# Opening of a hybrid layer kernel: plain transposes and a row of 1/rms in the first norm, dt products beside the first two column tiles, three small exponentials as one

## Chip, cores and metric

The kernel runs on one core of one Trainium2 chip. The metric is the device time of one execution in microseconds, the median of several runs. Engines are named as in the profile: PE (TensorE), DVE (VectorE), ACT (ScalarE), POOL (GpSimd), SP (the queue that issues most DMAs).

## What is computed

One layer of a decoder, for 1024 prompt tokens and 8 decode tokens (1032 rows): RMSNorm, one input projection, two groups of heads side by side (HGRN2 and a Mamba-2 SSD mixer), an output projection, then a gated MLP with a short convolution. The part that the change touches is the first norm, the B and C columns and the dt columns of the projection, and the small functions of dt and of the lower bound:

```python
h = rmsnorm(x, w['norm1_w'])
proj = h @ w['w_in']
...
xbc, buf_s_new = causal_dwconv(xbc_r, buf_s, w['ssm_conv_w'], w['ssm_conv_b'])
xbc = jax.nn.silu(xbc.astype(f32))
xs, Bm, Cm = jnp.split(xbc, [D_SSM, D_SSM + SSM_GROUPS * SSM_STATE], axis=-1)
dt = jax.nn.softplus(dt_r.astype(f32) + w['ssm_dt_bias'].astype(f32))
A = -jnp.exp(w['ssm_a_log'].astype(f32))
...
lb_all = jnp.cumsum(jax.nn.softmax(hgrn_lb.astype(jnp.float32), axis=0), axis=0)
```

## The kernel before

Activations are kept transposed, with features on partitions: `hT_hi[k]` and `hT_lo[k]` (tiles `hh` and `hl`) are the eight 128-feature blocks of the normed input, split into a rounded high part and a low remainder, each 1032 tokens wide. Every fp32 product is made of three reduced-precision ones (`hh` by `wh`, `hl` by `wh`, `hh` by `wl`) that accumulate in one PSUM bank. The tokens are walked in three chunks of 344, so that one 128-column tile of the projection costs 3 chunks by 8 blocks by 3 = 72 matmuls. `wload` (L180) loads a column tile of weights (`ws`), ACT rounds it (`wh`, L188) and DVE makes the remainder (`wl`, L189); each has two buffers. Product banks (`mm`, and `dt`) have three.

**The opening.** `first_norm` (L106) runs once for each chunk's group of three token tiles (`xt`, 128 tokens each; the ninth holds the 8 decode tokens). ACT squares and sums each tile in two halves (L115), DVE and ACT make 1/rms (L116 to L118), DVE multiplies an identity matrix by it (`dg`, L119). PE then multiplies each 128 by 128 block of `xt` by `dg` as an fp32 matmul, which transposes and scales in one (`tp`); such a matmul stands as two instructions in the trace. ACT scales by the norm weight and rounds (`hh`, L128), DVE makes `hl` (L129). After each group come the products of that chunk for two column tiles, one of B and one of C (L399 to L406). ACT copies each finished bank to `ext` (`xbc_evict`, L360), a tile of 1060 columns of which there are two buffers (tag `e`).

**After it.** Conv state rows are transposed (`cst`, L338), more norm vectors too (`vps`, L149). `xbc_close` (L368) makes the causal convolution of a column tile: ACT's Identity (L350), three DVE instructions (L352), then Silu on ACT (L374, L375). For the B and C tiles this is called at L424. Then come 48 `dt` matmuls (L433 to L438) into `dtr`, nine fp32 matmuls `dps` that turn dt back to tokens on partitions (L448), and on DVE a chain of some two dozen small instructions for softplus (`spx`, L464 to L480, with one Exp at L469), which ends with `av` (L484). PE needs `av` for `cps` (L486), the running sums of the SSD scan, from which the decay tiles `dec` and `csT` and the whole scan follow. Two more small Exps stand at L482 (`alog_bc`) and L757 (`lbt`). Four masks `lowf` are cut by POOL (L415) in a tile of tag `e`, and DVE copies them to `mlow` (L533).

**Order.** In the opening, on all engines, a scheduler of the framework orders the instructions by their dependences and its own costs, across the calls above. From L1122 on PE's order is the written one: the column tiles of the first x job (`x0`, weights `wh`, bank after bank) and so on to `x3`, `x7`, then the heads, the output projection and the MLP. The other engines stay with the scheduler.

## Time and profile before

| what | value |
|---|---|
| median of 3 runs | 1798.19 us (1797.17 to 1802.01) |
| profiled execution, first to last instruction | 1794.6 us |
| granted PE clock over it | 0.992 |
| busy: PE, DVE, ACT, POOL | 1741.0, 1116.6, 789.1, 409.8 us |
| HBM traffic | 100 GB/s over the span |

The page gives the busy time of each engine, its course over 40 slices, and the costliest groups of instructions. The timeline gives each instruction's start, its duration and, in brackets, the idle time before it and what ended that. Instructions of one engine overlap: a 344-wide matmul is shown with 0.32 us, but the next one starts 0.16 us later. The sum of what PE does is therefore read from starts, not from durations. The profiled span and the median of the runs differ by 3.6 us, which lie around the span.

### The profile page before, as it was taken

Reading aid. Unit: us, or ns where it says so; the run is one execution under the profiler, and the core shown is the slowest. Engines: PE = TensorE matmul, PEld = TensorE weight load, DVE = VectorE, ACT = ScalarE, POOL = GpSimd, SP = SyncE. Lnnn points to the kernel's source line nnn. Section 1 sums busy time; section 2 is a strip of 40 time slices with the busy share of each in tenths; the row PEclk is TensorE's granted clock in tenths of the full one; section 3 lists DMA queues with packets and bytes.
Section 4 is the critical chain, followed back from the end, with each engine's and each line's share of the span. In section 5 each row is a group of like instructions: output and inputs, shape, how many; then the busy total and the mean of one; then the engine's idle time right before and its main releaser. Section 6 shows DMA issues by size and latency. Waiting matters only on the chain.

```text
span 1794.6 us, 38584 instructions
## 1 busy us (share of the span) xinstructions
PE 1741.0 (97%) x16215; PEld 1685.0 (94%) x16215; DVE 1116.6 (62%) x2002; ACT 789.1 (44%) x1414; POOL 409.8 (23%) x415
## 2 busy tenths in 40 slices
PE   7999899999999999999999988999999999999998
PEld 7998798999999999999999978999999999999997
DVE  4658967556555564557746769666666667555545
ACT  6477688454544444345323344333433334111114
POOL 1103331110110110110100364455444542000001
PEclk9999999999999999999999998999999999999999
DMA  5135634553222221235334431222222225422212
GB/s 154 36 98 155 171 100 138 175 147 99 72 77 63 78 79 50 74 96 159 94 107 130 133 116 48 94 73 71 75 85 90 72 71 193 150 95 96 96 60 95
DMA packets 218018, 182.34 MB, mean 102 GB/s; under 512 B 13388, under 2 KB 195158, under 8 KB 217830
## 3 DMA queue, kind: packets, MB, share of 16 engines
q1 hardware_dynamic: 217558, 179.80, 32.5%
q8 instruction: 127, 2.08, 0.5%
q14 instruction: 45, 0.37, 0.1%
q0 software_dynamic: 288, 0.10, 0.0%
HBM read 141.53 MB, written 38.52 MB: 100 GB/s over the span
## 4 chain that ended last, share of the span: by engine, by line
PE 77%; DVE 8%; ACT 6%; DMA 5%; issue 2%; POOL 2%; SPq 0%; DVEq 0%; POOLq 0%; ACTq 0%
PE mm L93 30%; PE ub L93 14%; PE dn L93 13%; PE ua L93 10%; PE a L93 2%; PE o L93 1%; DMA csb<-cs_d 1%; ACT csb L549 1%; PE tp L93 1%; DVE wl L189 1%; DMA Bb<-bc_d 1%; PE kv L93 1%; DMA Sd<-in_state_ssm_dram 1%; DMA out_dram<-Sd 1%; DVE xbc L352 1%
## 5 line engine op out<-in xcount | busy, mean ns | idle before, releaser
L93 PE MATMUL mm<-hh,wh 128*128 128x344 f32 x1248 | 406.2, 326 | 2.6 <-ACT sz L685 2.6
L93 PE MATMUL mm<-hl,wh 128*128 128x344 f32 x1248 | 403.9, 324 | 0.0
L93 PE MATMUL mm<-hh,wl 128*128 128x344 f32 x1248 | 402.8, 323 | 0.0
L93 PEld LDWEIGHTS mm<-hh,wh 128*128 128x128 f32 x1248 | 234.6, 188 | 5.9 <-ACT sz L685 2.9
L93 PEld LDWEIGHTS mm<-hh,wl 128*128 128x128 f32 x1248 | 234.9, 188 | 2.4 <-issue 1.2
L93 PEld LDWEIGHTS mm<-hl,wh 128*128 128x128 f32 x1248 | 234.6, 188 | 2.5 <-issue 0.9
L188 ACT CAST wh<-ws 128x1024 fp32r<-128x1024 f32 x96 | 100.6, 1048 | 265.4 <-PE dn L93 135.8
L93 PE MATMUL ub<-ul,wh 128*128 128x258 f32 x704 | 199.6, 284 | 4.2 <-DVE ul L1182 4.2
L93 PE MATMUL ub<-uh,wh 128*128 128x258 f32 x704 | 201.1, 286 | 2.0 <-ACT uh L1181 2.0
L93 PE MATMUL ub<-uh,wl 128*128 128x258 f32 x704 | 200.8, 285 | 0.0
L93 PE MATMUL dn<-ah,wh 128*128 128x256 f32 (+1 forms) x640 | 180.7, 282 | 1.2 <-DVE x L1425 1.2
L93 PE MATMUL dn<-al,wh 128*128 128x256 f32 (+1 forms) x640 | 180.3, 282 | 0.0
L93 PE MATMUL dn<-ah,wl 128*128 128x256 f32 (+1 forms) x640 | 179.9, 281 | 0.0
L93 PE MATMUL mm<-mh,wh 128*128 128x258 f32 x512 | 148.2, 290 | 10.7 <-DVE x L1078 8.1
L189 DVE TENSOR_TENSOR wl<-ws,wh 128x1024 fp32r<-128x1024 f32 x96 | 125.3, 1306 | 52.5 <-ACT wh L188 52.3
L93 PE MATMUL ua<-ul,wh 128*128 128x258 f32 x528 | 148.9, 282 | 0.9 <-DVE ul L1182 0.9
L93 PE MATMUL ua<-uh,wl 128*128 128x258 f32 x528 | 149.4, 283 | 0.0
L93 PE MATMUL ua<-uh,wh 128*128 128x258 f32 x528 | 149.2, 282 | 0.0
L93 PE MATMUL mm<-ml,wh 128*128 128x258 f32 x512 | 146.5, 286 | 0.0
L93 PE MATMUL mm<-mh,wl 128*128 128x258 f32 x512 | 146.1, 285 | 0.0
L93 PEld LDWEIGHTS ub<-ul,wh 128*128 128x128 f32 x704 | 134.6, 191 | 4.9 <-DVE ul L1182 4.9
L93 PEld LDWEIGHTS ub<-uh,wh 128*128 128x128 f32 x704 | 134.2, 191 | 2.5 <-ACT uh L1181 2.5
(331 smaller groups left out, 3925.0 us busy)
## 6 DMA issues: line engine op xcount, KB each, us to landing
ws<-in_w_in_dram SPq DMA_DIRECT2D x52, 512.0 KB
ws<-in_w_up_dram SPq DMA_DIRECT2D x44, 512.0 KB
ws<-in_w_out_dram SPq DMA_DIRECT2D x24, 512.0 KB
act_d<-val SPq DMA_DIRECT2D x22, 516.0 KB
al<-act_d SPq DMA_DIRECT2D x22, 516.0 KB
ws<-in_w_down_dram SPq DMA_DIRECT2D x22, 512.0 KB
ml<-mix_d SPq DMA_DIRECT2D x48, 172.0 KB
csb<-cs_d SPq DMA_DIRECT2D x32, 256.0 KB
```

The lines of the kernel that those rows point to most:

```text
L93: PE.matmul(out, lhsT, rhs, start=start, stop=stop)
L188: A.copy(wh[:, :n], ws[:, :n])
L189: V.tensor_tensor(wl[:, :n], ws[:, :n], wh[:, :n].bitcast(F32), op=ALU.subtract)
L352: V.scalar_tensor_tensor(acc[:, :n], ext[:, q:q + n], col(wname, q * ntile + j), acc[:, :n], op0=ALU.mult, op1=ALU.add)
L549: A.activation(csb3[:, h, :], csb3[:, h, :], AF.Relu, scale=-1.0, bias=cst[:, h0 + h:h0 + h + 1])
```

## The change

**First norm.** `first_norm` goes. `turned` transposes a block of `xt` with the plain identity (`PE.transpose`), which needs no 1/rms. `Group` holds one chunk's statistics: the squares of the three tiles go to one tile, and sum, root, reciprocal and `dg` (three diagonals in one 128 by 384 instruction) are made once for a group. `rows` multiplies a matrix of ones by the diagonals: each row of the result `rb` holds 1/rms along the tokens, and ACT copies it to SBUF. `normed` multiplies the transposed block by the norm weight and by that row on DVE (`hn`), ACT rounds it to `hh`, and `low` subtracts on DVE (`hl`).

**dt.** The dt weights are loaded earlier (on SP ahead of token tiles 4 to 8), and the 16 dt matmuls of a chunk stand beside the products of the two column tiles (`products`); for the first chunk the products with `wl` and dt are held back three steps. The halves of `wl` are made between the steps of the norm.

**Order.** The whole opening is written out for PE, ACT and DVE. Step s turns block s, norms block s - 3 and multiplies block s - 4, over the 24 blocks of the three chunks.

**Exponentials.** The inputs of the three Exps are laid side by side in one tile of 176 columns with one Exp. The convolution of B and C (`xbc_close`) is issued only after that Exp; its Silus come 52 ticks of the job machine later. `sel`, `mlow`, `eyec`, `ones_r` and `selod` are issued only after the last `hl`.

```diff
-    def first_norm(tiles, then=()):
-
-        xs = []
-        for i in tiles:
-            xt, t0, n = xtm[i]
-            sq = half("xn")
-            ss = keep.tile([P, 4], F32, tag="ss", bufs=4, name=nm("ss"))
-            dg = tl("z", "dg")[:, :P]
-            for i in range(2):
-                A.activation(sq[:n], xt[:n, i * 512:(i + 1) * 512], AF.Square, accum_out=ss[:n, i:i + 1])
-            V.tensor_tensor(ss[:n, 2:3], ss[:n, 0:1], ss[:n, 1:2], op=ALU.add)
-            A.activation(ss[:n, 3:4], ss[:n, 2:3], AF.Sqrt, bias=epsc[:n], scale=1.0 / DM)
-            V.reciprocal(ss[:n, 3:4], ss[:n, 3:4])
-            V.tensor_scalar(dg[:n, :n], ident[:n, :n], ss[:n, 3:4], None, op0=ALU.mult)
-            xs.append((xt, dg, t0, n))
-        for work_ in then:
-            work_()
-        c0, c1 = xs[0][2], xs[-1][2] + xs[-1][3]
-        for k in range(KT):
-            tp = bank("tp")
-            for xt, dg, t0, n in xs:
-                mm(tp[:, t0 - c0:t0 - c0 + n], xt[:n, k * P:(k + 1) * P], dg[:n, :n])
-            A.activation(hT_hi[k][:, c0:c1], tp[:, :c1 - c0], AF.Copy, scale=col("n1", k))
-            V.scalar_tensor_tensor(hT_lo[k][:, c0:c1], tp[:, :c1 - c0], col("n1", k),
-                                   hT_hi[k][:, c0:c1].bitcast(F32), op0=ALU.mult, op1=ALU.subtract)
...
+    ones = keep.tile([P, P], F32, name="ones")
+    G.memset(ones, 1.0)
...
-        A.copy(ext[:, 3 + cs.start:3 + e], ps[:, :e - cs.start])
+        evicted[0] = A.copy(ext[:, 3 + cs.start:3 + e], ps[:, :e - cs.start])
...
-    def xbc_close(j, ext):
+    def xbc_close(j, ext, wait=0):
...
-        A.activation(acc[:, :T], acc[:, :T], AF.Silu)
-        A.activation(acc[:, T:NT], acc[:, T + 3:T + 32:4], AF.Silu)
+
+        def silu():
+            with tc.issue_after(evicted[0].ins):
+                A.activation(acc[:, :T], acc[:, :T], AF.Silu)
+                A.activation(acc[:, T:NT], acc[:, T + 3:T + 32:4], AF.Silu)
+
+        if wait:
+            after(wait, silu)
+        else:
+            silu()
...
+    wdt_s = tl("ld", "wdt_s")[:, :KT * 16].rearrange("p (k m) -> p k m", m=16)
+    wdt = tl("d", "wdt", F32R)[:, :KT * 32].rearrange("p (k m) -> p k m", m=32)
+    load_x(3)
+    SP.dma_start(wdt_s, w_in_[0, :, OFF_DT:OFF_DT + 16].rearrange("(k p) m -> p k m", p=P))
+    for i in range(4, 9):
         load_x(i)
     vec_cols(0)
-    for c in range(NCH):
-        first_norm(range(3 * c, 3 * c + 3), () if c else rounded)
-        for j, w, ext in first:
-            xbc_evict(j, ext, c, chunks[c], prod(w, 0, P, hT_hi, hT_lo, chunks[c]))
-
-
-    ones = keep.tile([P, P], F32, name="ones")
-    G.memset(ones, 1.0)
+    dtr = tl("g", "dtr")
+    G.memset(dtr[:, :NT], 0.0)
+
+    LAG = 4
+    NS = NCH * KT
...
+        def square(self, i):
+            xt, t0, n = self.tiles[i]
+            junk = half("xn")
+            for q in range(2):
+                A.activation(junk[:n], xt[:n, q * 512:(q + 1) * 512], AF.Square, accum_out=self.sq[:n, q, i:i + 1])
...
+        def stats(self):
+            ss = self.ss
+            V.tensor_tensor(ss[:, 0:3], self.sq[:, 0, 0:3], self.sq[:, 1, 0:3], op=ALU.add)
+            A.activation(ss[:, 0:3], ss[:, 0:3], AF.Sqrt, bias=epsc, scale=1.0 / DM)
+            V.reciprocal(ss[:, 0:3], ss[:, 0:3])
+            self.dg = tl("z", "dg").rearrange("p (a t) -> p a t", t=P)
+            V.tensor_tensor(self.dg, ident.unsqueeze(1).to_broadcast([P, 3, P]),
+                            ss[:, 0:3].unsqueeze(2).to_broadcast([P, 3, P]), op=ALU.mult)
+
+        def rows(self):
+            rb = bank("rb", "nx")
+            for i, (xt, t0, n) in enumerate(self.tiles):
+                mm(rb[:, t0 - self.c0:t0 - self.c0 + n], ones[:n], self.dg[:n, i, :n])
+            self.rows_ = tl("z", "rows")
+            A.copy(self.rows_[:, :self.w], rb[:, :self.w])
...
+    def turned(s):
+        g, k = groups[s // KT], s % KT
+        tps[s] = bank("tp")
+        for xt, t0, n in g.tiles:
+            PE.transpose(tps[s][:, t0 - g.c0:t0 - g.c0 + n], xt[:n, k * P:(k + 1) * P], ident[:n, :n])
+
+    def low(u):
+        g, k = groups[u // KT], u % KT
+        return V.tensor_tensor(hT_lo[k][:, g.cs], hns.pop(u), hT_hi[k][:, g.cs].bitcast(F32), op=ALU.subtract)
+
+    def normed(u):
+        g, k = groups[u // KT], u % KT
+        hn = half("hn")[:, :g.w]
+        V.scalar_tensor_tensor(hn, tps.pop(u)[:, :g.w], col("n1", k), g.rows_[:, :g.w], op0=ALU.mult, op1=ALU.mult)
+        A.copy(hT_hi[k][:, g.cs], hn)
+        hns[u] = hn
+        if u:
+            low(u - 1)
...
+    beside = {0: lambda: weight_high(1), 1: lambda: weight_low(0, 0), 2: lambda: weight_low(1, 0),
+              3: dt_weight, 4: lambda: weight_low(0, 1), 5: lambda: weight_low(1, 1)}
...
+        if c == 0 and k < KT - 1:
+            now = [(0, 0), (1, 0), (0, 1), (1, 1)]
+            held.append((k, [(0, 2), (1, 2), (2, 0), (2, 1)]))
+            for w in now:
+                first_mm(c, w, k, k == 0 and w[1] == 0, False)
+            if len(held) > 3:
+                kk, ws_ = held.pop(0)
+                for w in ws_:
+                    first_mm(c, w, kk, kk == 0 and w == (2, 0), False)
+            return
+        for i, ws_ in enumerate(parts):
+            for kk, hw in held:
+                for w in hw:
+                    if w[0] == i:
+                        first_mm(c, w, kk, kk == 0 and w == (2, 0), False)
+            for w in ws_:
+                first_mm(c, w, k, k == 0 and w[1] == 0, k == KT - 1 and w == ws_[-1])
+            if k == KT - 1:
+                if i < 2:
+                    xbc_evict(first[i][0], first[i][2], c, chunks[c], accs[i])
+                else:
+                    A.copy(dtr[:32, chunks[c]], accs[2])
...
+    with tc.manual_schedule(engines={mybir.EngineType.PE, mybir.EngineType.Activation, mybir.EngineType.DVE}):
+        groups.append(Group(0))
+        for i in range(3):
+            groups[0].square(i)
+        groups[0].stats()
+        weight_high(0)
+        for s in range(NS + LAG):
+            if s < NS:
+                turned(s)
+            u = s - LAG + 1
+            if 0 <= u < NS:
+                c, k = divmod(u, KT)
+                if k == 0:
+                    groups[c].rows()
+                normed(u)
+                if u in beside:
+                    beside[u]()
+                if c + 1 < NCH:
+                    if k == 1:
+                        groups.append(Group(c + 1))
+                    if k in (1, 3, 4):
+                        groups[-1].square((1, 3, 4).index(k))
+                    if k == 5:
+                        groups[-1].stats()
+                if u == NS - 1:
+                    settled = low(u)
+            if s >= LAG:
+                products(s - LAG)
...
-    BT[0], CT[0] = (xbc_close(j, ext) for j, w, ext in first)
...
+    with tc.issue_after(settled.ins):
+        V.tensor_tensor(sel, ident[:, 0:16], ident[:, 16:32], op=ALU.add)
...
+    xx, ee_al, s1, s2 = (tl("z", "spx")[:, :NDT + 32] for i in range(4))
+    V.tensor_tensor(lbt[:, 0, :], vcol[:, lo0:lo0 + 8], vcol[:, lo1:lo1 + 8], op=ALU.max)
+    V.tensor_tensor(ee_al[:, NDT + 16:NDT + 24], vcol[:, lo0:lo0 + 8], lbt[:, 0, :], op=ALU.subtract)
+    V.tensor_tensor(ee_al[:, NDT + 24:NDT + 32], vcol[:, lo1:lo1 + 8], lbt[:, 0, :], op=ALU.subtract)
+    V.tensor_copy(ee_al[:, NDT:NDT + 16], alog_bc)
+    xx, ee, s1, s2 = (t[:, :NDT] for t in (xx, ee_al, s1, s2))
...
+    least = V.tensor_tensor(ee, ee, xx, op=ALU.min)
+    expd = A.activation(ee_al, ee_al, AF.Exp)
+    with tc.issue_after(least.ins), tc.issue_after(expd.ins):
+        BT[0], CT[0] = (xbc_close(j, ext, 52) for j, w, ext in first)
+    V.tensor_scalar(alog_bc, ee_al[:, NDT:NDT + 16], -1.0, None, op0=ALU.mult)
+    V.tensor_tensor(lbt[:, 3, :], ee_al[:, NDT + 16:NDT + 24], ee_al[:, NDT + 24:NDT + 32], op=ALU.add)
+    V.reciprocal(lbt[:, 3, :], lbt[:, 3, :])
+    V.tensor_tensor(lbt[:, 0, :], ee_al[:, NDT + 16:NDT + 24], lbt[:, 3, :], op=ALU.mult)
+    V.tensor_scalar(lbt[:, 1, :], lbt[:, 0, :], -1.0, 1.0, op0=ALU.mult, op1=ALU.add)
...
-    A.activation(alog_bc, alog_bc, AF.Exp)
-    V.tensor_scalar(alog_bc, alog_bc, -1.0, None, op0=ALU.mult)
...
-    V.tensor_tensor(lbt[:, 0, :], vcol[:, lo0:lo0 + 8], vcol[:, lo1:lo1 + 8], op=ALU.max)
-    V.tensor_tensor(lbt[:, 1, :], vcol[:, lo0:lo0 + 8], lbt[:, 0, :], op=ALU.subtract)
-    V.tensor_tensor(lbt[:, 2, :], vcol[:, lo1:lo1 + 8], lbt[:, 0, :], op=ALU.subtract)
-    A.activation(lbt[:, 1:3, :], lbt[:, 1:3, :], AF.Exp)
...
```

**Where instructions move (1).** DVE at the seam between the first and the second chunk of tokens. `hl_9` to `hl_16` are the low parts of blocks 0 to 7, `hn` the normed block ahead of its split; `rows_50` and `rows_77` hold the rows of 1/rms of the first and the second group. Before:

```order
L129 SCALAR_TENSOR_TENSOR hl_16_96<-tp_52_225,vcol_99,hh_8_88 128x384
L119 TENSOR_SCALAR dg_63_303<-ident_107,ss_62_302 128x128
L116 TENSOR_TENSOR ss_75_411<-ss_75_411 128x1
L118 RECIPROCAL ss_75_411<-ss_75_411 128x1
L116 TENSOR_TENSOR ss_78_420<-ss_78_420 128x1
```

And now, the same place:

```order
L444 SCALAR_TENSOR_TENSOR hn_72_303<-tp_62_240,vcol_99,rows_50_199 128x384
L439 TENSOR_TENSOR hl_14_94<-hn_69_281,hh_6_86 128x384
L444 SCALAR_TENSOR_TENSOR hn_74_319<-tp_65_257,vcol_99,rows_50_199 128x384
L439 TENSOR_TENSOR hl_15_95<-hn_72_303,hh_7_87 128x384
L444 SCALAR_TENSOR_TENSOR hn_78_341<-tp_68_277,vcol_99,rows_77_339 128x384
L439 TENSOR_TENSOR hl_16_96<-hn_74_319,hh_8_88 128x384
```

The last low part of a chunk, `hl_16`, now stands behind `hn_78`, the first instruction that reads the next group's row. That row comes from three matmuls `rb` on PE, which stand behind the products of the block before.

**Where instructions move (2).** ACT around the evictions of x0. `ext_126` (now `ext_147`) takes the three banks of x0; `wh_132_890` (now `wh_153_930`) is the weight tile of x2, in the buffer that x0 reads; `spx` is the Exp; `xbc` written from `ext` is the Identity that begins a convolution. Before:

```order
L374 ACTIVATE xbc_102_585<-xbc_102_585 128x1024
L375 ACTIVATE xbc_102_585<-xbc_102_585 128x8
L469 ACT_TABLE_LOAD
L469 ACTIVATE spx_111_676<-spx_111_676 128x144
L362 COPY ext_126_799<-mm_127_801 128x344
L362 COPY ext_126_799<-mm_128_827 128x344
L188 CAST wh_132_890<-ws_131_889 128x1024
L362 COPY ext_126_799<-mm_129_853 128x336
```

And now:

```order
L588 ACT_TABLE_LOAD
L588 ACTIVATE spx_130_702<-spx_130_702 128x176
L323 ACTIVATE xbc_133_714<-ext_24_131,vcol_99 128x1056
L323 ACTIVATE xbc_134_720<-ext_28_137,vcol_99 128x1056
L164 CAST wh_153_930<-ws_152_929 128x1024
L337 COPY ext_147_835<-mm_148_837 128x344
L337 COPY ext_147_835<-mm_149_863 128x344
L352 ACT_TABLE_LOAD
```

The two Identities of B and C moved behind the Exp, the Silus behind x0's first evictions, and the rounding of x2's weights ahead of those evictions.

**Where instructions move (3).** DVE between dps and the softplus chain. Before, the six conv instructions (`xbc`) stand ahead of the first instruction that reads `dps`:

```order
L352 SCALAR_TENSOR_TENSOR xbc_101_577<-ext_24_129,vcol_99,xbc_101_577 128x1056
L352 SCALAR_TENSOR_TENSOR xbc_102_585<-ext_28_135,vcol_99,xbc_102_585 128x1056
L447 MEMSET dps_109_656 128x16
L533 CAST mlow_761<-lowf_124_756 32x128 x4
L464 TENSOR_TENSOR spx_110_675<-dps_109_656,bias_bc_667 128x144
L758 TENSOR_TENSOR lbt_773<-lbt_773 128x8
L467 TENSOR_SCALAR spx_111_676<-spx_110_675 128x144
```

And now, where the first half of the softplus chain, from `dps` to a reciprocal, stands ahead of the six conv instructions, of which the last two are shown:

```order
L325 SCALAR_TENSOR_TENSOR xbc_133_714<-ext_24_131,vcol_99,xbc_133_714 128x1056
L325 SCALAR_TENSOR_TENSOR xbc_134_720<-ext_28_137,vcol_99,xbc_134_720 128x1056
L594 TENSOR_TENSOR lbt_700<-spx_130_702,lbt_700 128x8
L598 TENSOR_TENSOR spx_131_703<-spx_131_703,spx_130_702 128x144
L595 TENSOR_SCALAR lbt_700<-lbt_700 128x8
L659 CAST mlow_806<-lowf_145_801 32x128
L599 TENSOR_TENSOR spx_132_704<-spx_131_703 128x144
```

The conv now splits the softplus chain in two, and the first `mlow`, which waits for POOL's masks, stands inside the chain.

91 lines of the change are left out of this document (53 added, 38 removed).

## Prediction

> **What bounds the kernel now.** First the page: how much of the span PE has work.
>
> ```profile
> span 1794.6 us, 38584 instructions
> PE 1741.0 (97%) x16215; PEld 1685.0 (94%) x16215; DVE 1116.6 (62%) x2002; ACT 789.1 (44%) x1414; POOL 409.8 (23%) x415
> ```
>
> PE is the bound: a microsecond of work taken off it counts, unless a wait takes its place. Next the windows, stage by stage (length, then busy time of PE, PEld, DVE, ACT, POOL).
>
> ```profile
> 19.50:65.00 45.50, 45.50 (x311) 41.15 (x309) 22.18 (x55) 24.35 (x54) 0.34 (x2) 1.00 0.21 55
> 65.00:120.00 55.00, 55.00 (x352) 54.14 (x351) 31.70 (x70) 36.48 (x58) 4.80 (x14) 1.00 0.21 55
> 120.00:200.00 80.00, 77.45 (x545) 70.94 (x544) 67.05 (x110) 62.07 (x134) 24.76 (x27) 1.00 0.56 160
> 200.00:250.00 50.00, 44.51 (x298) 40.34 (x297) 40.31 (x70) 38.04 (x79) 16.06 (x11) 0.97 0.49 132
> ```
>
> The opening (to about 65) and the x jobs up to 120 keep PE busy without a gap, DVE and ACT only half so. So the change's stage has nothing to win but PE work, and every new wait is a loss. From 120 to 250, 8.0 us of waits follow. Then PE's timeline at the joints (start, duration):
>
> ```profile
> 9.77 2.50 PE L93 MATMUL tp<-dg,xt 128*128 128x128 f32 x10 [3.67 <-DVE dg L119]
> 25.86 4.85 PE L93 MATMUL tp<-dg,xt 128*128 128x128 f32 x42
> 38.91 7.60 PE L93 MATMUL tp<-dg,xt 128*128 128x128 f32 x48
> 59.75 0.32 PE L93 MATMUL dt<-hl,wdt 128*32 128x344 f32 x1
> 59.90 0.32 PE L93 MATMUL dt<-hh,wdt 128*32 128x344 f32 x1
> 63.34 1.19 PE L93 MATMUL dps<-sel,dtr 128*128 128x16 f32 x10
> 64.37 0.40 PE L93 MATMUL mm<-hh,wh 128*128 128x344 f32 x1
> 69.33 0.21 PE L93 MATMUL dps<-sel,dtr 128*8 128x16 f32 x2
> 76.83 0.32 PE L93 MATMUL mm<-hh,wh 128*128 128x344 f32 x1
> 85.66 0.46 PE L93 MATMUL cps<-av,tri 128*128 128x128 f32 x2
> 1760.82 1.91 PE L1450 MATMUL fin<-ident,x 128*128 128x128 f32 x16
> ```
>
> x0 starts at 64.37, and x1 at 76.83 (72 matmuls and the last dps further) without a gap.
>
> **Part one, the norm on PE.** A transposing matmul by `dg` is two instructions, 4.85 / 42 = 0.115 us each, 0.23 together. A plain transpose is one, 1.91 / 16 = 0.12. The first two groups have 48 blocks: 48 x 0.11 = 5.3 us less. The third group takes 7.60 / 8 = 0.95 per block; with four instructions of 0.115, its 8-row tile takes 0.49, of which a transpose saves half or nothing: 8 x (0.23 to 0.48) = 1.8 to 3.8 less. Added: nine `rb` matmuls, 0.23 each and 0.49 for the 8-row one, 2.3. Net about 6 us of PE work less. The 48 dt matmuls move but stay (0.15 apart).
>
> Whether that arrives depends on what paces PE. For that, ACT and DVE rows:
>
> ```profile
> 8.76 0.19 ACT L115 ACTIVATION_READ_ACCUMULATOR xn<-xt 128x1 f32 x1
> 13.45 0.58 ACT L128 ACTIVATE hh<-tp,vcol 128x384 fp32r<-128x384 f32 x1
> 76.88 1.05 ACT L188 CAST wh<-ws 128x1024 fp32r<-128x1024 f32 x1 [3.18 <-PE mm L93]
> 10.94 1.23 DVE L189 TENSOR_TENSOR wl<-ws,wh 128x1024 fp32r<-128x1024 f32 x1 [0.52 <-ACT wh L188]
> 28.54 0.28 DVE L430 TENSOR_TENSOR wdt<-wdt_s,wdt 128x128 fp32r<-128x128 f32 x1
> 30.68 2.88 DVE L129 SCALAR_TENSOR_TENSOR hl<-tp,vcol,hh 128x384 fp32r<-128x384 f32 x5 [0.30 <-ACT hh L128]
> 33.47 0.60 DVE L119 TENSOR_SCALAR dg<-ident,ss 128x128 f32<-128x128 f32 x3
> ```
>
> DVE did one 384-wide instruction a block (2.88 / 5 = 0.58) and now does two. The squares of the third tile end at 8.95; sum, root, reciprocal and a 384-wide `dg` (1.2 in all), `rb` (six instructions at the 0.25 of the first row above), the copy (0.5), the first `hn` and its rounding (1.1) bring the first product to about 13.6. From 12.4 on DVE has, up to the seventh `hl`, 15 x 0.58 + four half `wl` (half of 1.23 each) + `wdt` 0.28 + the next group's statistics 0.9 = 12.3 us: that `hl` is there at 24.7. PE's work in that time is less than 9 us; DVE paces the first chunk. Then the seam: six products (0.95), a block's transposes (0.35), three `rb` (0.7), ACT's copy (0.5), `hn` (0.58), and only then the eighth `hl` (0.58): 28.4 and some handoffs, against PE out of work at about 27. So 1.5 us of wait, and the same at the next seam. The rest: 2.4 us to end the first chunk, then 64 products (0.157) with four old and four new blocks' transposes and `rb` (14 to 16 with the seam's wait 1.5 more), then 64 products with four blocks (11.5 to 13). Last, x0's bank is free only when ACT has done a rounding of 1.05, held until PE's last read of the first `wh`, and evictions behind it: another 0.8. Together x0 starts at 60 to 62; I take 61.2. By my sum most of the 6 us goes into DVE's pace and the two seams.
>
> Equal footing: in x0 now lie all 18 dps instructions (10 took 1.03 before, so 1.85), two groups of four small transposes (0.9 by the 0.12 each) and two vector ones (0.2). x0's PE work is 72 x 0.158 + 2.95 = 14.3, so it ends at 75.5, against 76.83: **-1.3 us**.
>
> **Part two, the seam from x0 to x1.** Rows for the chain behind dps:
>
> ```profile
> 71.98 0.33 ACT L469 ACTIVATE spx<-spx 128x144 f32<-128x144 f32 x1 [1.99 <-DVE spx L468]
> 72.21 0.43 ACT L362 COPY ext<-mm 128x344 f32<-128x344 f32 x1
> 60.03 7.46 DVE L352 SCALAR_TENSOR_TENSOR xbc<-ext,vcol,xbc 128x1056 f32<-128x1056 f32 x6 [0.76 <-ACT xbc L350]
> 70.07 0.93 DVE L533 CAST mlow<-lowf 32x128 uint8<-32x128 f32 x4 [2.49 <-POOL lowf L415]
> 72.34 0.24 DVE L470 TENSOR_SCALAR spx<-spx 128x144 f32<-128x144 f32 x1
> 72.61 1.05 DVE L471 RECIPROCAL spx<-spx 128x144 f32<-128x144 f32 x1
> 74.10 0.31 DVE L473 TENSOR_TENSOR spx<-spx 128x144 f32<-128x144 f32 x1
> 85.20 0.31 DVE L484 TENSOR_TENSOR av<-dt,alog_bc 128x144 f32<-128x144 f32 x1
> L415 POOL TENSOR_SCALAR_AFFINE_SELECT lowf<-ones 128x128 f32<-128x128 f32 x4 | 3.6, 932 | 8.6 <-DVE xbc L352 8.6
> ```
>
> Before, the conv ran from 60.03 to 67.49 under the dt matmuls, both `ext` buffers were free, and x0's first bank left at 72.21, 4.6 us ahead of need. Now the conv waits for the Exp, the Exp for dps, and dps stands 28 products and the small transposes inside x0: it ends 7.4 us after x0's start, at 68.6. Three small DVE steps and the Exp (1.3), three small ones and the reciprocal (1.5) and six conv instructions (7.46) reach 78.9. One `ext` buffer goes to `lowf`; the other comes free with the last conv. ACT, in order, holds all evictions of x0 behind that, and x1's first product needs x0's first bank (three banks). So x1 starts at 78.9 + 0.5 = 79.4, against PE free at 75.5: **+3.9 us**. If the `ext` buffers did not bind, the rounding for x2, which waits for x0's last read and now stands ahead of the evictions, would still cost 1.05 + 0.43 = 1.5.
>
> **Part three, cps.** `lowf` starts with the fifth conv instruction's end, 77.7, and takes POOL 3.6: 81.3. The first `mlow` in DVE's queue waits for it, and the rest of the softplus chain stands behind. From 74.10 to 85.51 that rest took 11.4 before (with x2's `wl` and x0's conv among it, as now): `av` is there at about 92.8. PE comes to cps 56 products after x1's start, 79.4 + 8.8 = 88.2. Before, `av` came 0.15 ahead of cps. Now **+4.6 us**; without the mask in the chain it would be 2.4.
>
> **Part four, the Exps.** One Exp of 176 columns for three; two table loads fewer in the whole program. Their rows:
>
> ```profile
> 28.66 1.28 ACT L482 ACT_TABLE_LOAD   x1
> 29.96 0.21 ACT L482 ACTIVATE alog_bc<-alog_bc 128x16 f32<-128x16 f32 x1
> ```
>
> ACT is half idle there and PE had no gap: 0. [...]
>
> **The sum.** -1.3 + 3.9 + 4.6 = 7.2 us; with x0 at 62.2 it is 8.2, at 60 it is 6.0. All three terms are new waits on chains that follow x0's start. Behind cps, the chain of waits runs over ACT and a load of the running sums that cps makes, and is back on PE at 221:
>
> ```profile
> 85.06 1.28 ACT L374
> 98.31 8.17 DMA csb<-cs_d
> 221.24 11.35 PE mm L93 x72
> ```
>
> So a late cps is mostly passed on; where PE was delayed by more than that chain, up to a us or so is taken back from the 8.0 of waits there. I forecast +6.3: 1794.6 + 6.3 + 3.6 around the span = 1804.5, the median of 1798.2 plus 6.3.
>
> **Rivals.**
> *The waits are absorbed.* PE lost 3.9 at the seam, and meanwhile DVE, ACT, POOL and the loads went on, so that half of the 8.0 us of waits up to 250 go. For it: those waits end on DVE and ACT. Against: these engines wait on cps too. 7.2 - 4 = +3: 1801. Chance 0.22.
> *The opening keeps its 6 us.* DVE does the 384-wide steps faster than its old 0.58 (SBUF alone for `hl`), the seams hide, and the banks do not bind at x1. Then -6 plus the 1.5 of the rounding, -4.5: 1793.7; wholly without waits 1792.2. For it: DVE was half idle in the window from 19.5. Against: the order puts the conv behind the Exp. It decides if the first `ext` of x0 comes before 75.5. Chance 0.13.
> *PE stays at half pace longer.* The transposes before 12.6 took 0.25 each, those from 25.86 on 0.115. In the new order PE starts with transposes and gaps, so the slow pace might last into the products up to 25: about 9 us of work would take up to twice as long, of which DVE's pace hides some 5: +3, in all +9.5: 1807.7. [...] Chance 0.12.
>
> **Numbers.** The forecast has the remaining 0.53. Some 0.3%, 5.4 us, is what a measurement here can tell from no change. The forecast's own range is 1802.5 to 1806.5; a fifth of it lies within the 5.4. Same: 0.10 + 0.20 (absorbed) + 0.04; slower: 0.43 + 0.02 + 0.12; faster: 0.09. The range reaches from the absorbed case's lower side, 1798, to the slow clock's upper, 1809.5.
>
> **What would show it.** Right: PE's first products at 13 to 15; two waits of 1 to 2 us on `hl` at about 27 and 45; x0 at 60 to 62; a wait of about 4 before x1 on ACT's `ext`, that on DVE's conv; one of about 4.6 before cps on `av`; `mlow` waiting for `lowf` inside the chain. Wrong: x1 without a wait, `av` ahead of PE, or the lag at 250 under 3 us.

## The result and the profile after

| | before | after |
|---|---|---|
| median | 1798.33 us (1797.17 to 1802.01, 4 runs) | 1814.97 us (1813.78 to 1817.73, 4 runs) |
| profiled span, granted PE clock | 1794.6 us, 0.992 | 1814.1 us, 0.989 |

The ratio is 1.0089 (95% interval 1.007 to 1.0107): 16 us slower, between 12.6 and 19.3. The forecast was 1804.5, range 1798.0 to 1809.5: the sign was right, the size less than half. In one kernel below (the kernel before with only the second part of the change) two of the twelve executions, of 2399.33 and 6622.31 us, count as slow and are not in its median. The page of the changed kernel has nearly the same PE work (1743.7 against 1741.0) in a span 19.5 us longer, so most of what came is waiting:

```profile
span 1814.1 us, 38478 instructions
PE 1743.7 (96%) x16161; PEld 1684.9 (93%) x16161; DVE 1122.2 (62%) x2014; ACT 785.6 (43%) x1407; POOL 408.5 (23%) x415
```

Its windows (length; busy time of PE, PEld, DVE, ACT, POOL; granted PE clock; DMA share; GB/s):

```profile
19.50:65.00 45.50, 41.80 (x268) 35.87 (x266) 25.26 (x66) 21.84 (x52) 0.00 (x0) 1.00 0.16 44
65.00:120.00 55.00, 47.73 (x280) 46.47 (x280) 34.83 (x74) 29.47 (x47) 5.14 (x16) 0.91 0.19 52
80.00:85.00 5.00, 4.77 (x21) 4.77 (x22) 3.10 (x12) 4.35 (x8) 2.62 (x8) 0.67 0.00 0
95.00:100.00 5.00, 5.00 (x20) 4.94 (x20) 0.72 (x3) 3.67 (x8) 0.00 (x0) 0.50 0.01 3
```

In the second window PE now stands 7.3 us of 55, where it had no gap, and the clock is 0.91 where it was 1.00. The last two rows cut out the stretches where it drops; nothing in the prediction's sum stood for them.

PE's timeline of the changed kernel at the joints (start, duration, in brackets the wait):

```profile
13.86 0.64 PE L93 MATMUL mm<-hh,wh 128*128 128x344 f32 x1
23.64 0.57 PE L93 MATMUL mm<-hl,wh 128*128 128x344 f32 x2 [0.71 <-DVE hl L439]
29.11 0.43 PE L93 MATMUL mm<-hl,wh 128*128 128x344 f32 x1 [1.05 <-DVE hl L439]
46.64 0.43 PE L93 MATMUL mm<-hl,wh 128*128 128x344 f32 x1 [1.11 <-DVE hl L439]
61.52 0.42 PE L93 MATMUL mm<-hh,wh 128*128 128x344 f32 x1 [0.84 <-ACT dtr L503]
80.23 0.65 PE L93 MATMUL mm<-hh,wh 128*128 128x344 f32 x1 [3.58 <-ACT ext L337]
80.68 0.49 PE L93 MATMUL mm<-hl,wh 128*128 128x344 f32 x1
80.97 0.49 PE L93 MATMUL mm<-hh,wl 128*128 128x344 f32 x1
94.39 0.76 PE L93 MATMUL cps<-av,tri 128*128 128x128 f32 x2 [3.68 <-DVE ddx L631]
232.42 0.63 PE L738 MATMUL sT<-ident,S 128*128 128x128 f32 x4 [3.58 <-DVE S L713]
408.08 1.51 PE L93 MATMUL ms<-gacc,ones 128*128 128x344 f32 x2 [2.87 <-DVE vd L959]
871.14 0.75 PE L93 MATMUL a<-q,k 128*32 128x32 f32 x64 [3.89 <-DVE q L992]
1778.36 1.91 PE L1565 MATMUL fin<-ident,x 128*128 128x128 f32 x16
```

x1 (80.23) is 3.4 us later than before, cps (94.39) 8.7. Behind each of the two waits, products start 0.29 us apart (80.68, 80.97) and not 0.16. The last four rows are later than the same instructions of before by 12.0, 13.1, 14.7 and 17.5 us (the first three of these are in the next fence). Before had these there:

```profile
220.39 0.63 PE L613 MATMUL sT<-ident,S 128*128 128x128 f32 x4 [2.00 <-DVE S L588]
394.97 0.85 PE L93 MATMUL ms<-gacc,ones 128*128 128x344 f32 x2 [0.67 <-DVE vd L844]
856.48 0.76 PE L93 MATMUL a<-q,k 128*32 128x32 f32 x64
```

So three waits far behind the change grew as well, by 1.6, 2.2 and 3.9 us. The other engines of the changed kernel at the seam from x0 to x1, and before cps:

```profile
72.28 7.36 DVE L325 SCALAR_TENSOR_TENSOR xbc<-ext,vcol,xbc 128x1056 f32<-128x1056 f32 x6
76.53 1.04 ACT L164 CAST wh<-ws 128x1024 fp32r<-128x1024 f32 x1 [3.35 <-PE mm L93]
79.73 0.79 ACT L337 COPY ext<-mm 128x344 f32<-128x344 f32 x2 [2.16 <-DVE xbc L325]
78.55 3.63 POOL L541 TENSOR_SCALAR_AFFINE_SELECT lowf<-ones 128x128 f32<-128x128 f32 x4 [12.81 <-DVE xbc L325]
82.22 0.23 DVE L659 CAST mlow<-lowf 32x128 uint8<-32x128 f32 x1 [1.54 <-POOL lowf L541]
93.93 0.31 DVE L608 TENSOR_TENSOR av<-dt,alog_bc 128x144 f32<-128x144 f32 x1
```

The conv ends at 79.64 and ACT copies x0's bank at once, which lets x1 start; `lowf` keeps POOL till 82.2, and `mlow`, inside the softplus chain, waits for it. Both chains are those of the prediction.

### The profile page after: what moved, and what is told of

Its sections match the earlier page's. It is cut to its first block, busy times and chain, and to the rows that moved or that the text cites. A ratio compares the mean times of both kernels' runs of the same rounds, so it can differ in the third digit from the quotient of the medians.

```text
span 1814.1 us, 38478 instructions
## 1 busy us (share of the span) xinstructions
PE 1743.7 (96%) x16161; PEld 1684.9 (93%) x16161; DVE 1122.2 (62%) x2014; ACT 785.6 (43%) x1407; POOL 408.5 (23%) x415
## 4 chain that ended last, share of the span: by engine, by line
PE 76%; DVE 9%; DMA 5%; ACT 5%; issue 3%; POOL 2%; SPq 0%; DVEq 0%; POOLq 0%; ACTq 0%
PE mm L93 30%; PE ub L93 14%; PE dn L93 13%; PE ua L93 10%; PE a L93 2%; PE o L93 1%; DMA csb<-cs_d 1%; DVE xbc L325 1%; ACT csb L674 1%; DVE wl L165 1%; PE kv L93 1%; DMA out_dram<-Sd 1%; DMA Bb<-bc_d 1%; POOL Cb L777 1%; ACT L675 0%
## 5 line engine op out<-in xcount | busy, mean ns | idle before, releaser
L93 PE MATMUL mm<-hh,wh 128*128 128x344 f32 x1248 | 411.5, 331 | 5.3 <-ACT ext L337 3.6
```

Source lines behind the costliest of these rows:

```text
L93: PE.matmul(out, lhsT, rhs, start=start, stop=stop)
```

## The experiments

"Lag" is how much later PE starts an instruction than the first profile of the kernel before starts the same one; that profile's execution was some 2 to 4 us quicker than the medians of its kernel (1798.3 to 1800.4 in the batches here): in every execution with both figures the time is 1.65 to 2.35 us above the span, so that the 3.6 us between its 1794.6 and the median do not all lie around the span. Dummy products are products that nobody reads. Theory A at the start: the chains of the prediction are right, and a half pace behind each standstill and later losses come on top. Rivals: the new edge that holds the conv behind the Exp costs by itself, or the mask does.

**The conv at its old place** (B and C, ahead of dps, Silus at once):

```diff
+    BT[0], CT[0] = (xbc_close(j, ext) for j, w, ext in first)
...
-    with tc.issue_after(least.ins), tc.issue_after(expd.ins):
-        BT[0], CT[0] = (xbc_close(j, ext, 52) for j, w, ext in first)
```

> The changed kernel, with the convolution of the B and C tiles issued where it stood before, ahead of dps, and its Silus at once (no waiting for the joint Exp). Theory A (the queues behind dps): the conv no longer waits for the Exp, but the dt products no longer lie behind the opening to cover it. It starts at about 66, with the vectors, so the masks come at about 77, the Exp behind them at 78, and ACT still holds x0's first eviction behind the Exp: the wait before x1 stays 2.5 to 4 us, the one before cps falls from 3.7 to about 2. In all 1 to 3 us less than the changed kernel: 1812 to 1814. Rival B (tying the conv to the Exp is by itself the cause): the wait before x1 goes, and with it 7 to 11 us: 1804 to 1808.

Measured: 1811.65 us, ratio 1.0058 (1.0046 to 1.007). The wait before x1 stays (3.96 us), that before cps falls from 3.68 to 0.65. ACT in this run:

```profile
65.93 2.43 ACT L323 ACTIVATE xbc<-ext,vcol 128x1056 f32<-128x1056 f32 x2 [3.78 <-DVE vcol L124]
79.62 0.35 ACT L589 ACTIVATE spx<-spx 128x176 f32<-128x176 f32 x1 [1.07 <-DVE spx L588]
79.88 1.12 ACT L337 COPY ext<-mm 128x344 f32<-128x344 f32 x3
```

Without the edge the conv's Identity waits for a transposed vector until 65.93, and x0's evictions now stand behind the Exp. `av` comes 1.3 us sooner (92.61), and PE's order now has 66 products between x1 and cps, where the change had 56; the lag at 112 us falls from 11.3 to 5.7. So the edge costs a part of the time behind x1; at x1 itself another chain of the same length takes its place, since the dt products no longer stand there for the conv to hide under. The rival that the edge alone is the cost falls.

**The mask out of the chain** (`mlow` only behind `av`):

```diff
-            V.tensor_copy(mlow[rows], lowf[rows, :, rows])
+            with tc.issue_after(av_.ins):
+                V.tensor_copy(mlow[rows], lowf[rows, :, rows])
```

> The changed kernel, with the four mlow copies issued only after av, so that the softplus chain on DVE does not wait for POOL's masks. Theory A: the wait before x1 stays 3.6 us; the wait before cps falls from 3.7 to 1.5 to 2, and the half-pace stretch of PE behind it (2.5 us lost) goes or halves: 2 to 4.5 us less than the changed kernel, 1810.5 to 1813. Rival (the chain of small DVE instructions is late whatever stands in it): no more than 0.5 us less.

Measured: 1815.66 us, 1.009 (1.0078 to 1.0102). A miss: Theory A's 2 to 4.5 us did not come. The wait before cps is gone, but PE waits a little further on, and the half pace behind x1 is twice as long (granted clock 0.51 from 80 to 85 us and 0.80 to 90, against 0.67 and then 1.00; timeline, then a window of this run):

```profile
98.37 0.18 PE L634 MATMUL dd<-ident,ddx 8*32 8x8 f32 x1 [2.25 <-ACT csT L625]
```

```profile
80.00:85.00 5.00, 4.11 (x14) 4.12 (x15) 4.76 (x13) 4.58 (x8) 4.07 (x6) 0.51 0.30 83
```

**PE kept busy through the two waits** (23 dummy products ahead of x1, 15 about cps; nothing is left out):

```diff
+    def warm(n):
+        wm = bank("wm")
+        for i in range(n):
+            mm(wm[:, :CH], hT_hi[0][:, :P], hT_hi[0][:, chunks[0]])
```

> The changed kernel, with 38 matmuls added whose result nobody reads: 23 ahead of x1's first product and 15 around cps, where PE stood still. They fill the waits and shorten none. Theory A with the clock (a standstill of 3.6 us costs PE's full pace for the next 3.4 or 6.8 us): x1 and cps come within 0.4 us of where they came (80.2 and 94.4), products behind both are 0.158 us apart instead of 0.287, so PE's lag at 100 is 2 to 2.6 us smaller; 1 to 3 us less than the changed kernel: 1812 to 1814. Rival (the half pace comes from elsewhere, or added work costs its time): the half pace stays at 80 and 95, and the kernel takes 0 to 6 us more.

Measured: 1812.36 us, 1.0067 (1.0055 to 1.0079). Its timeline, then its windows:

```profile
77.05 3.69 PE L93 MATMUL wm<-hh 128*128 128x344 f32 x23
80.79 0.42 PE L93 MATMUL mm<-hh,wh 128*128 128x344 f32 x1
...
94.96 0.76 PE L93 MATMUL cps<-av,tri 128*128 128x128 f32 x2 [3.35 <-DVE ddx L638]
```

```profile
80.00:85.00 5.00, 4.95 (x32) 4.68 (x32) 3.10 (x12) 4.66 (x9) 2.96 (x7) 1.00 0.00 0
95.00:100.00 5.00, 5.00 (x25) 4.98 (x26) 0.72 (x3) 4.66 (x9) 0.00 (x0) 0.72 0.00 0
```

Where PE had dummy work instead of a wait, x1 runs at clock 1.00, 32 products in the window where the change had 21. At cps, where the dummies did not close the gap, half the slow stretch remains (clock 0.72 from 95 to 100, against 0.50). So in these two runs the pace goes with the standstill. But it is not a cost everywhere: from x1 to cps PE takes 14.17 us here and 14.16 in the change. In both, as in the kernel before, cps starts 0.46 us behind the start of `av`; at full pace PE only waits longer for it. The lag at 112 us is hardly less than the change's (11.1 against 11.3; x0 came half a microsecond later); that part of the expectation failed.

**The seam** (the last `hl` of a group ahead of the next group's rows):

```diff
-        if u:
+        if u % KT:
...
+                    if c:
+                        low(u - 1)
```

> The changed kernel, with the last low part of a chunk issued ahead of the next group's rows, on DVE and PE, at the two seams of the opening. Theory A: the two waits of 1.1 us on hl go; x0, x1 and cps each come 2 to 2.5 us sooner, since the chain behind dps starts from x0, and the two large waits stay as long as they are: 2 to 2.5 us less, 1812.5 to 1813. Rival C (the conv, the masks or the loads set x1 and cps by times of their own): x0 comes sooner, x1 and cps do not, the large waits grow by 2: within 0.5 us of the changed kernel.

Measured: 1812.36 us, 1.0065 (1.005 to 1.008). The waits on `hl` fall from 2.9 to 0.4, x0 starts at 59.43, and the two waits behind it stay:

```profile
78.14 0.65 PE L93 MATMUL mm<-hh,wh 128*128 128x344 f32 x1 [3.57 <-ACT ext L337]
92.31 0.77 PE L93 MATMUL cps<-av,tri 128*128 128x128 f32 x2 [3.76 <-DVE ddx L633]
```

Both chains hang on x0's start, as the prediction had it: all comes 2.1 us sooner.

**The parts apart.** The first kernel has the dt products behind the two column tiles with the conv under them, but the new norm and the joint Exp; the second is the kernel before with only the joint Exp, the conv behind it and the late Silus; the third is the first with the seam's edit.

```diff
-            held.append((k, [(0, 2), (1, 2), (2, 0), (2, 1)]))
+            held.append((k, [(0, 2), (1, 2)]))
...
+    BT[0], CT[0] = (xbc_close(j, ext) for j, w, ext in first)
+    for c, cs in enumerate(chunks):
+        ps = psmm.tile([P, 512], F32, tag="mm", name=nm("dt"))
+        for k in range(KT):
+            mm(ps[:32, :CH], wdt[:, k, :], hT_hi[k][:, cs], start=(k == 0), stop=False)
+            mm(ps[:32, :CH], wdt[:, k, :], hT_lo[k][:, cs], start=False, stop=(k == KT - 1))
+        A.copy(dtr[:32, cs], ps[:32, :CH])
```

> The changed kernel with the 48 dt products behind the first two column tiles again and the conv of B and C under them, as before; the new first norm, its written-out order and the joint Exp stay. Theory A: the two large waits (before x1 and before cps) go, and with them the half-pace stretches; what is left is the opening alone, in which the 6 us of saved PE work are eaten by DVE's pace in the first chunk and three waits of 1.2 to 1.6 us: x1 starts within 1 us of before (76.8), the kernel takes 0 us more or less than before, within 2. Rival (the new opening saves its 6 us, and the conv and its queues cost 20): 4 to 6 us less than before. Rival (the new opening itself costs): 4 to 10 us more than before.

> The kernel before with only the second part of the change: the joint Exp, the conv of B and C tied behind it and the late Silus; opening and dt stay as they were. Theory A: dps ends at 65 to 66 here, so the same chain ends sooner against x1 (76.8): a wait of 1 to 2 us before x1 and 1 to 2 before cps, no half pace behind waits that short: 2 to 4 us more than before. Rival (the order tied to the Exp costs what the whole change costs): 9 us and more above before. Rival (harmless without the new opening): within 1 us of before.

> The same as the run with the dt products behind, with the last low part of a chunk also ahead of the next group's rows at the two seams. Theory A: the seams give 2 to 2.5 us; x1 starts at 74.5 to 75, and no wait takes their place, so 2 to 2.5 us less than that run, 1 to 3 less than before. Rival C (a wait of fixed time at x1 or cps takes it back): as that run.

Measured: the first 1808.54 us, 1.0041 (1.0023 to 1.0059); the second 1803.88, 1.0019 (1.0002 to 1.0036); the third 1803.92, 1.0017 (1.0002 to 1.0032), against 1799.19 for the kernel before. The first is outside Theory A's 2 us, within the rival's 4 to 10; the third, expected 1 to 3 us below before, is above it. The second fits Theory A, and has both waits, though smaller:

```profile
80.52 0.43 PE L93 MATMUL mm<-hh,wh 128*128 128x344 f32 x1 [1.32 <-ACT ext L364]
93.48 0.46 PE L93 MATMUL cps<-av,tri 128*128 128x128 f32 x2 [2.13 <-DVE ddx L528]
```

So the late conv hurts also where dt stands at its old place; and the half pace that Theory A did not expect there comes behind the wait of 2.13 us (clock 0.71 from 95 to 100). The first shows that the new norm alone wins nothing: between 110 and 140 us its lag is 0.3 to 0.5, its waits on `hl` come to 4.2 us in five. And it shows something that no theory had: without a wait of note up to 140, its lag is 4.0 at 300 us and 9.8 at 1100.

**All repairs together, dt beside the tiles** (the seam's edit, the conv right behind the opening, the mask behind `av`, and the small transposes inside the last chunk):

```diff
+            if s - LAG in (17, 18, 19):
+                next(cols, 0)
+            if s - LAG in (20, 21):
+                vec_cols(s - LAG - 19)
...
+    BT[0], CT[0] = (xbc_close(j, ext) for j, w, ext in first)
```

> The changed kernel with the dt products beside the column tiles, as changed, and three repairs: the last low part ahead of the next group's rows at the seams; the conv state's transposes and the two vector transposes in the written-out order of the last chunk, so that the conv of B and C starts right behind the opening (about 62) and dps ahead of x0; the mlow copies behind av. Theory A: the conv ends at 70, x0's evictions and av come in time; waits of 0 to 1 us before x1 and before cps, x1 at 72 to 73.5 although all of x0's small work is done by then: 3 to 5 us less than before. Rival (the opening is bound by DVE, and more in its last chunk makes it slower): x0 not before 63, no gain over before.

Measured: 1802.24 us, ratio 0.9998 (0.9981 to 1.0014): not told from the kernel before, and 12.7 us below the change by the medians. The 3 to 5 us below before that Theory A expected did not come. The stage that was lost is mended:

```profile
65.00:120.00 55.00, 54.14 (x344) 52.98 (x343) 36.28 (x73) 33.90 (x57) 6.22 (x16) 1.00 0.23 64
```

It is 4.3 us ahead of before at 120 us, level at 400 and 3.3 behind at 1100. What it gains early it loses later, too.

**Is it lateness that loses?** The kernel before once more, unchanged; with 70 and with 20 dummy products between two products of x2, from 100 us on (the expectations say x3 and 115 us), PE's other instructions in their old order; and with the load of the dt weights as early as in the change (`ones` earlier as well).

```diff
+    after(200, lambda: warm(70))
```

```diff
+    load_x(3)
+    SP.dma_start(wdt_s, w_in_[0, :, OFF_DT:OFF_DT + 16].rearrange("(k p) m -> p k m", p=P))
+    for i in range(4, 9):
         load_x(i)
```

> The kernel before once more, unchanged, to learn how far two profiles of one kernel differ along the way. If the later losses of the change (at 160 to 230, 330 to 400 and 860 us) are a matter of chance between executions, this profile shows losses of several us against the first one at some of these places, and its span is 2 us or more longer than 1794.6. If they belong to the change, it stays within 1 us of the first profile all along. Time within 2 us of the other runs of the kernel before.

> The kernel before with 70 products that nobody reads put between two products of x3, at about 115 us, and every instruction else in its old place: TensorE is late by 70 times 0.152 us, about 10.6, as it is in the change at this point. Theory A (lateness alone changes what later transfers and vector steps meet, and these cost another 5 to 8 us): 16 to 19 us over the kernel before, with waits for S, vd and q such as the change shows. Theory B (the later losses come with the change's own instructions or their order): 10 to 11.5 us over, and a lag that stays level from 130 us on. Theory C (other engines have slack and take part of the delay back, as the prediction's third part thought of a microsecond): 6 to 9.

> As the run with 70 unread products, with 20: TensorE 3.0 us late at 115 us. Theory A: 3 us plus some of the later losses, 4.5 to 9 over the kernel before. Theory B: 2.5 to 3.5. Theory C: 0 to 2.

> The kernel before with only the load of the dt weights issued ahead of the fourth and later row tiles, as in the change, and the ones set earlier on GpSimd; the sums and their order on the other engines are as before. Theory B in the form that the order of the early transfers carries the later losses: 4 to 7 us over the kernel before. Theory A: within 1.5 us of it, with x0 at 63 within half a microsecond.

Measured against 1800.35: unchanged 1798.69, 1.0002 (0.9991 to 1.0013); 70 dummies 1813.77, 1.0087 (1.0066 to 1.0108); 20 dummies 1806.14, 1.0036 (1.0021 to 1.0051); the transfers 1799.25, 0.9996 (0.9984 to 1.0008). The dummies put PE 11.1 and 3.15 us back; the kernels are 11.9 to 19.4 and 3.8 to 9.2 us slower (by the medians 13.4 and 5.8). So a kernel with dummies loses more than they take. That this is lateness alone is not shown:

- Both profiles were 2.4 and 2.2 us late before the first dummy product (the unchanged repeat 0.5): the third token tile came 0.6 to 1.0 us later, and the first products, up to 17 us, took another 1.2. That is as much as the medians have above the 11.1 and 3.15; whether every execution of these kernels has it is not known.
- The scheduler gave ACT, DVE and POOL another order between 100 and 257 us, as it did in the change.
- The early dt load costs nothing. But the change also issues two copies of convolution state at 16 and 22 us; in the transfer run, as in the kernel before, they are issued at 28 and 29. The change's whole order of early transfers is not tested.

The lags of all these profiles:

| kernel | lag at 112 us | at the last product |
|---|---|---|
| before, unchanged | 0.5 | 1.5 |
| before, early dt load | 1.0 | 4.0 |
| before, only the second part of the change | 7.5 | 7.3 |
| before, 20 dummies; 70 dummies | 5.3; 13.5 | 11.6; 18.8 |
| the change | 11.3 | 19.0 |
| the change, dt behind; and with the seam's edit | 0.5; -1.5 | 12.4; 7.4 |
| the change, all repairs | -3.1 | 6.0 |

Lateness at 112 us is neither needed for the later losses nor enough for them. The old opening with the late conv is 7.5 us late and loses nothing more. Three kernels with the new opening are on time or ahead and lose 9 to 12; in the two with dt behind, PE, DVE, ACT and POOL run the very order of the kernel before from 112 us on. By the medians these two are 9.3 and 4.7 us above before. So Theory B does not fall: the profiles, one of each kernel, point to something of the new opening that costs time later, and no run here shows what it is. The early state copies are one candidate that is left.

Three of the later waits, one by one. First row, unchanged kernel; second, 70 dummies:

```profile
220.79 0.63 PE L613 MATMUL sT<-ident,S 128*128 128x128 f32 x4 [3.59 <-DVE S L588]
```

```profile
409.84 0.85 PE L93 MATMUL ms<-gacc,ones 128*128 128x344 f32 x2 [3.00 <-DVE vd L850]
```

The changed kernel's 3.58 before `sT` thus comes in the old kernel too, by chance; it needs nothing of the change. Its 2.87 before `ms` comes with 70 dummies (3.00), and with dt behind, at a lag of 2.9 (3.04). And its 3.89 before `a` comes with 20 dummies; here is that run with POOL, DVE and PE:

```profile
859.46 1.04 POOL L863 TENSOR_TENSOR vb<-vb,k 128x512 f32<-128x512 f32 x1 [12.40 <-PE a L93]
859.85 0.69 DVE L885 TENSOR_TENSOR tt<-tt 128x32 f32<-128x32 f32 x1
860.58 1.54 POOL L865 TENSOR_TENSOR Sh<-Sh,vb 128x512 f32<-128x512 f32 x1
860.89 1.26 DVE L885 TENSOR_TENSOR tt<-tt 128x16 f32<-128x16 f32 x1
863.95 1.75 DVE L883 TENSOR_TENSOR q<-q,tt 128x512 f32<-128x512 f32 x1
865.85 1.08 PE L93 MATMUL a<-q,k 128*32 128x32 f32 x64 [3.79 <-DVE q L883]
```

Two small DVE steps end within 0.05 us of the POOL steps that had begun ahead of them. The same steps in the kernel before:

```profile
853.74 0.17 DVE L879 TENSOR_TENSOR tt<-tt 128x32 f32<-128x32 f32 x1
853.84 0.50 DVE L1018 TENSOR_TENSOR ml<-ml,mh 128x344 fp32r<-128x344 f32 x1
853.95 3.01 POOL L857 TENSOR_TENSOR vb<-vb,k 128x512 f32<-128x512 f32 x1 [13.01 <-DMA vb<-vd_d]
854.27 0.16 DVE L879 TENSOR_TENSOR tt<-tt 128x16 f32<-128x16 f32 x1
856.32 0.67 DVE L879 TENSOR_TENSOR tt<-tt 128x8 f32<-128x8 f32 x1
857.34 1.77 DVE L876 TENSOR_TENSOR k<-k,tt 128x512 f32<-128x512 f32 x1
```

There DVE's `tt` of 32 columns began 0.2 us ahead of POOL, and DVE was in its next step (`ml`) when POOL came; it was POOL that took 3.01, against the 1.04 above. DVE steps took longer only later (`tt` of 8 columns 0.67 us, `k` 1.77 against 0.67), where PE did not wait for them. It goes by this order in the six kernels compared for it. PE waits 3.79 to 3.89 us before this `a` in the three where POOL came 0.3 to 0.4 us ahead of that `tt` (20 dummies, all repairs, the change), and at most 1.0 in the three where POOL came 0.2 to 0.8 us behind it (the kernel before, the one with only the second part of the change, the one with dt behind). How late PE is does not decide it: that `tt` comes 2.4 us sooner to 11.3 us later than in the kernel before in the first three, 0 to 7.5 later in the others. With all repairs, 3.1 us ahead just before it, the wait comes too:

```profile
857.32 0.75 PE L93 MATMUL a<-q,k 128*32 128x32 f32 x64 [3.83 <-DVE q L996]
```

**Those POOL steps left out.** The kernel with 20 dummies, the changed one and the one before, each without the four POOL steps of the last HGRN head (`vb` times `k`, `Sh` plus `vb`, twice), so that head's decode state and what comes of it lack a term:

```diff
-                G.tensor_tensor(d4(vb), d4(vb), cb(k[:, ds]), op=ALU.mult)
+                if h < H - 1:
+                    G.tensor_tensor(d4(vb), d4(vb), cb(k[:, ds]), op=ALU.mult)
...
-                G.tensor_tensor(Sd, Sd, vb, op=ALU.add)
+                if h < H - 1:
+                    G.tensor_tensor(Sd, Sd, vb, op=ALU.add)
```

> The kernel before with 20 unread products as in the run before, and without the four GpSimd steps that update the decode state of the last HGRN head (vb times k, Sh plus vb, twice), so that head's sampled state lacks one term. If these steps slow the VectorE chain tt, k, q when they fall on it, the wait of the product a for q at 866 (3.8 us) goes to under 0.5, the chain's tt 128x16 is back from 1.26 to 0.16 us, and the loss between 850 and 870 (4.1 in the profile of the run with the steps) goes; time 2.5 to 4.5 us under that run, so 1 to 4 over the kernel before. If it is something else that comes with the lateness (a transfer, the order), the wait and the 4.1 stay and the time is that of the run with the steps.

> The changed kernel without the same four GpSimd steps of the last head. If they carry the loss at 860: a<-q wait at 871 from 3.9 to under 0.5, lag behind the kernel before from 16.0 to 11 to 13 at 880, time 3 to 5 us under the changed kernel, 1810 to 1812. If not: 1814 to 1816.

> The control: the kernel before without the four steps. There they fell on a k and a q that no product waited for at once; so 0 to 1 us under the kernel before. If leaving them out helps here by 3 or more as well, their cost has nothing to do with the lateness.

Measured against 1799.67: 1802.57, 1.0009 (0.9993 to 1.0025) with 20 dummies; 1813.36, 1.0069 (1.0044 to 1.0095) for the change; 1798.36, 0.9983 (0.9965 to 1.0002) for the kernel before. With 20 dummies:

```profile
859.63 0.16 DVE L887 TENSOR_TENSOR tt<-tt 128x16 f32<-128x16 f32 x1
861.56 0.75 PE L93 MATMUL a<-q,k 128*32 128x32 f32 x64 [0.28 <-DVE q L885]
```

The wait goes from 3.79 to 0.28, and the lag at 880 us from 10.5 to 4.9; there these steps carry the loss. In the changed kernel they carry the wait (q is back to 0.69 us), but the lag at 880 falls only from 16.0 to 14.0, since 2.1 us of other loss came at 850; the expected time, 1810 to 1812, was missed. In the times neither gain is told from none: the intervals overlap with those of the kernels that have the steps.

## Why the prediction was wrong

The prediction's steps, in the order of the timeline:

| step | predicted | measured |
|---|---|---|
| first products | 13 to 15 | 13.86 |
| x0 starts; wait before it | 61.2 (60 to 62); 0.8 | 61.52; 0.84 |
| waits on `hl` | two of 1 to 2 | 1.05 and 1.11, and one of 0.71 |
| part one: PE free for x1, against before | 75.5, -1.3 | 76.65, -0.2 |
| part two: wait before x1; x1 | 3.9; 79.4 | 3.58; 80.23 |
| half pace from x1 to cps | not in the sum | 1.65, within the wait for `av` |
| part three: wait before cps; end of `av` | 4.6; 92.8 | 3.68; 94.24 |
| lag at cps | 7.2 | 8.7 |
| half pace behind cps | not in the sum | 2.5 |
| lag at 112 us | 7.2 | 11.3 |
| from there on | -0.9 | +8.2 in these two profiles, some 5 by the medians |

*What was right.* Parts one to three, as mechanisms: the DVE pace, the seams, the conv behind the Exp, the `ext` buffers, the mask in the chain. The four runs of the first batch moved these waits one by one, and each moved as the chain says, but for the mask's, where the next wait was already there. Part one was 1.1 us too kind, mostly because x0's stage took 15.1 and not 14.3 us.

*First failed step: "The sum".* It has 7.2 us at cps and no cost behind it; measured are 8.7 and 11.3. One part is a term that was too small: the path to `av` took 1.4 us longer than summed, as the conv ended 0.7 late, POOL's masks 0.9, and the rest of the softplus chain took 12.1 and not 11.4 us. The other is a term that the sum put at nothing, since it priced each wait at its length: having stood for 3.68 us, PE came back at half pace (clock 0.50 from 95 to 100 us, products 0.29 us apart). From cps to the same later product (`bc`, at 112 us before) it took 28.87 us without a wait, against 26.34: 2.5 us. In the run with dummy products the pace goes with the standstill: where they filled the gap, at x1, the slow stretch is gone (clock 1.00 from 80 to 85, against 0.67); where 3.35 us of a gap were left, at cps, half of it stays (0.72 from 95 to 100, against 0.50). From x1 to cps PE was slow too (10.48 us without the wait, against 8.83), but that only shortened the wait for `av`, which set cps either way. The rival "PE stays at half pace longer" had this mechanism, but at the start of the kernel, and there it was hidden: the products from 15.2 to 18 did run at half pace (0.29 us apart, from 18.5 on 0.16), under DVE's, and x0 came on time. That rival asked what pace would do in the opening, and never what the forecast's own two waits would do to it. A half pace came behind the waits of 3.58 and 3.68; the run with only the late conv shows one behind a wait of 2.13 too, and the run with the mask moved none behind 2.25 (clock 1.00 from 95 to 105).

*Second failed step: "up to a us or so is taken back".* It took the waits up to 250 for slack. They gave 1.2 us back by 130 (the lag fell from 11.3 to 10.1), but the lag was 13.5 at 240, of which the wait before `sT` is chance. Later places lost more: it rose from 10.9 to 13.8 about `ms`, from 10.7 to 16.0 about `a` (the wait of 3.89 and a half pace of 1.3 behind it, clock 0.60 from 871 to 875), and by 1.4 in the last transposes, with 2.6 and 2.4 given back ahead of `ms` and `a`. The waits further down were thus no slack. What sets them is shown for `a`: whether POOL's steps or DVE's come first, by some tenths of a microsecond; without POOL's steps the wait is gone (0.28 us with 20 dummies). For the rest the cause stays open: a late PE is not it by itself (7.5 us late, and nothing more lost, in the old opening with the late conv), and kernels with the new opening lose 9 to 12 us without it. Also shown is that the first profile of before was a lucky one (its unchanged repeat lagged by 1.5 at the end, and the one with the early dt load by 4.0, with no difference in the times), so that of the 19.5 us some 3 are the two profiles' own. Left open too: what holds `ms`, which no run isolates, and the 2.1 us at 850 in the run of the change without the POOL steps.

*The other rivals.* "Absorbed" fell: nothing was. "The opening keeps its 6 us" fell at its named point: the first `ext` of x0 came at 79.73, not before 75.5. (`hl`, now from SBUF alone, took 0.55 us by its median, 0.61 before.)

## What to carry to other kernels

Price a wait of a PE that has no gap as its length plus any slow stretch that the trace shows behind it, and ask what that stretch meets: here it cost 2.5 us where no wait followed, and nothing where the next wait was longer than it. Ask of each new wait whether other products could stand in it. When work is moved off a place, ask first what it covered there: behind the opening the dt products hid a conv of 7.4 us. And do not count on waits further down to take a delay back. Profile the old kernel twice before later differences are put down to a change, and compare the other engines' orders before a run with dummy work is read as lateness alone.

## What the hardware showed beside that

In the two profiles of the result all eleven stretches at a granted clock of 0.5 that ended within the span lasted 3.41 us or two or three times that. In the changed kernel it stood there from 79.88 to 83.29 us, about x1, and from 93.53 to 100.36, about cps. Within each of the two profiles they also began whole steps of 3.41 us apart: in the changed kernel at 79.88 and 233.48, 45 steps. It went by how much of one step PE stood idle: from 20 us on, up to the last 30, a step at clock 1.00 was always followed by a slow one when PE had stood 1.92 us of it or more, and never when it had stood less than 1.62. In the experiments the starts of the steps are an estimate from the windows' clocks. With the mask moved (0.51 from 80 to 85, 0.80 to 90) the slow stretch began at 80.1, and the wait of 2.25 (96.12 to 98.37) fell on two steps, 1.08 and 1.17; with only the late conv (0.95 from 90 to 95, 0.71 to 100) it began at 94.5, and the wait of 2.13 (91.35 to 93.48) lay within one. Products of 344 columns in the changed kernel were 0.287 us apart behind x1's start, up to 83, against 0.158 after it.

Some DVE and POOL steps that fell together took longer here. With 20 dummies a DVE step of 128 by 16 took 1.26 us beside POOL's steps and 0.16 without them, one of 128 by 512 took 1.75 and 0.67. In the kernel before, where DVE's steps had begun first, it was a POOL step that took 3.01, against 1.04 with 20 dummies, where POOL had begun first. Which of the two came first, by some tenths of a microsecond, went with PE's wait before `a` in the six kernels above: 3.79 to 3.89 us or at most 1.0.
